# Seven products for four pairs of k tiles in every unit of the projections and the MLP, plain pieces between them, and the residual kept in device memory

## The chip, the cores and the metric

The kernel runs on one core of a Trainium2 chip. The core has five engines that run side by side, each through its own instructions in order: TensorE (PE, matrix products), VectorE (DVE), ScalarE (ACT), GpSimd (POOL), SyncE (SP, which here only issues transfers). They work on an on-chip memory of 128 partitions; matmul results go to PSUM, of which a bank holds 128x512 float32. The metric is the time of one execution on the device in microseconds, the slowest core's, here the only one's.

## The reference

One block of a model on 256 rows of 2048 columns, in float32: a mixer of two branches (a gated linear recurrence and chunked attention), merged by two sigmoid gates, an output projection and an MLP with squared ReLU, each with a residual.

```python
z = u @ w_in                                   # u = rms_norm(x); queries, keys, values, gates
gate_a, gate_b = jnp.split(jax.nn.sigmoid(gates), 2, axis=-1)
merged = gate_a * (y_a @ w_branch_a) + gate_b * (y_b @ w_branch_b)
h = x + merged @ w_out
u = rms_norm(h, norm_mlp_w)
h = h + jnp.square(jax.nn.relu(u @ w_up)) @ w_down    # w_up 2048x8192, w_down 8192x2048
return rms_norm(h, norm_final_w)
```

## The kernel before

**Products in three passes.** A float32 operand is split into a rounded high part and the rest (`split`, L88 to L90: a cast on ScalarE, a subtraction on VectorE), and a product is three matmuls, high x high, high x low and low x high (`mm3`, L142 to L145). A weight piece holds two k tiles of 128 rows by 512 columns, 128x1024 on the chip; `piece` (L643) loads it on the SP queue, `parts` (L658) splits it. Before a matmul can run, its piece must have landed in a buffer `raw`, gone through the cast into `wh` and through the subtraction into `wl`.

**Stages.** The recurrence and the attention come first (to about 395 us) and are not touched. From there on the work is cut into 21 *units*, calls of `gemm_s` (L689), each a product of 256 rows (two halves m) with 2048 k rows (16 k tiles) and 1024 columns (two halves n): three for gates (`ga2`, `gb0`, `gb2`), then after the branch products (`gemm2`, L675, not units) two for the output projection (`wo0`, `wo2`), and four times, for a quarter of the MLP's width, two up (`up00`, `up02`, then `up10` and so on) and two down (`dn00`, `dn02`). A unit's four results (m, n), called 11, 12, 21, 22, gather in four banks; there are six banks (`ps_k`).

**Seven products for eight.** A unit plain is 2 x 2 x 16 triples of matmuls, 192. For a pair of k tiles (k, k + 4) the rows' halves, the columns' halves and the two k tiles make a 2 x 2 by 2 x 2 block product, done with seven products in place of eight (Winograd's form of Strassen's method). It needs four sums of left-hand blocks (S5, S4, S2, S7, made by `combos`, L586, with their own splits) and four sums of weight blocks, made in place in the raw buffers on VectorE (`add`, L711; `less`, L716). The banks exchange partial results: a bank is begun as a copy of another (`begun`, L747), and copies u1, u2 of bank 21 (`copy`, L744) are subtracted from 12 and 22 later (`more`, L756). The parameter r tells how many pairs are so done: 4 in the down units, 3 in the gates, in wo0 and in seven up units, 2 in wo2 and up00. With r = 3 the third pair comes in half pieces (X, Y). The rest of the k tiles go plain, `plains`, for both m and one n at a time. One plain piece (the last) is left to the next unit (`late`, `flush`).

**Order and buffers.** Tile, the layer below, orders each engine's instructions at build time by a priority and puts in the waits. Splits, weight sums, copies and evictions are raised (`tc.high_priority(offset=2000)`); transposes of the next stage's operand and the left-hand sums (`h_blocks`, `turns`, `turned`, handed in as `steps` and taken up at points of the unit) are not. Raw buffers are eight (six in `wpool`, two in `xp`), split halves six each. A unit loads its blocks W11, W12, W22, W21 first and each plain piece where it is used, all on SP's queue. Row tiles of 128x512 ("tokens", `token`, L575, 17 of them) hold gates, copies u1 and u2, MLP rows on their way and, from L949 on, the eight tiles of the residual h, in place to the end: x is loaded, `evict` (L685) adds the output projection on VectorE, and the down units' results go through ScalarE into a token y and are added into h by a transfer that accumulates, on POOL's queue (L1000). The last quarter's results are evicted into h directly, and then come the final norm and the stores.

Of the kernel before, what the change touches and what calls it, by code (L numbers as in the profile page):

```python
# [50 lines left out]
def tile_hybrid_block(  # L51
# [455 lines left out]
    TOK = 17  # L507
# [67 lines left out]
    def token(what):  # L575
        return tk.tile([P, NC], F32, name=what, tag="t", bufs=TOK)

# [6 lines left out]
    R = 3  # L584

    def combos(lhs, what, home, blocks=None, n=R):  # L586

        a = blocks
        if not a:
            a = []  # L590
            for m in range(NM):
                for j in range(2):
                    t = tk.tile([P, R, P], F32, name=f"a{m}{j}_{what}", tag="t", bufs=TOK)
                    x = lhs[j][:, :R, :, m * P:(m + 1) * P].bitcast(F32)
# [12 lines left out]
        for two in ((5, s5), (4, s4)), ((2, s2), (7, s7)):  # L607
            if n > R:
                more = tk.tile([P, 2, 2, P], F32R, name=f"S{two[0][0]}m_{what}", tag="t", bufs=TOK)
            for q, (i, s) in enumerate(two):  # L610
                t = (tk if home == "a" else xp).tile([P, R, 2, P], F32R, name=f"S{i}_{what}", tag=f"S{i}{home}", bufs=1)
                split(t[:, :, 0, :], t[:, :, 1, :], s[:, :R])
                made[i] = [[t[:, k, u, :] for u in range(2)] for k in range(R)]
                if n > R:
                    split(more[:, q, 0, :], more[:, q, 1, :], s[:, R])
                    made[i].append([more[:, q, u, :] for u in range(2)])
        return made

    Sx = combos(xT, "x", "a")
# [9 lines left out]
    xp = ctx.enter_context(tc.tile_pool(name="xpool", bufs=1, reuse_waits="tile"))  # L629
    ps_k = ctx.enter_context(tc.tile_pool(name="ps_k", bufs=6, space=PSUM, reuse_waits="tile"))  # L630
# [3 lines left out]
    taken = {t: 0 for t in BUFS}  # L634

    def buf(tag, dtype, what):

        old, new = BUFS[tag]
        first = taken[tag] % (old + new) < old
        taken[tag] += 1  # L640
        return (wpool if first else xp).tile([P, 2 * NC], dtype, name=f"{tag}_{what}", tag=tag, bufs=old if first else new)

    def piece(w, what, *halves):  # L643

        raw = buf("raw", F32, what)
        (n0, k0), (n1, k1) = halves
        ncols = w.shape[-1]
        kpr = 4 * NC // ncols
        if n0 == n1 and k1 == k0 + 1 and k0 // kpr == k1 // kpr:
            src = w[n0 // ncols:(n0 + NC) // ncols, k0 // kpr, :, k0 % kpr:k0 % kpr + 2, :].rearrange("c p a n -> p c a n")  # L650
            nc.sync.dma_start(raw.rearrange("p (c a n) -> p c a n", a=2, n=ncols), src)
            return raw, ncols < NC
        for i, (n, k) in enumerate(halves):
            nc.sync.dma_start(raw[:, i * NC:(i + 1) * NC].rearrange("p (c n) -> p c n", n=ncols),
                              w[n // ncols:(n + NC) // ncols, k // kpr, :, k % kpr, :].rearrange("c p n -> p c n"))
        return raw, False

    def parts(raw, what, half=None):  # L658

        raw, turned = raw  # L660
        made = [buf(t, F32R, what) for t in ("wh", "wl")]
# [4 lines left out]
        if half is not None:  # L666
            dst, src = [t[:, half * NC:(half + 1) * NC] for t in made], raw[:, half * NC:(half + 1) * NC]
# [7 lines left out]
    def gemm2(lhs, w, n0, nkt, what):  # L675

        acc = [bank(f"{what}{m}") for m in range(NM)]
        for k in range(0, nkt, 2):
            wh, wl = parts(piece(w, f"{what}{k}", (n0, k), (n0, k + 1)), f"{what}{k}")
# [9 lines left out]
    def gemm_s(lhs, S, w, n0, what, done, r=R, kt0=0, steps=(), start=4, fresh=False, tail=False):  # L689

        n1 = n0 + NC
        steps = list(steps)
        points = [0]

        def point():
            points[0] += 1  # L700
            if points[0] > start and steps:
                steps.pop(0)[1]()

        c = {}
        load = lambda name, *halves: piece(w, f"{what}{name}", *[(n, kt0 + k) for n, k in halves])
        groups = (0, 2) if r == 4 else (0,)
        four = lambda name, n, k: [load(f"{name}{g}", (n, k + g), (n, k + g + 1)) for g in groups]

        def add(dst, t):
            with tc.high_priority(offset=2000):  # L710
                nc.vector.tensor_tensor(dst, dst, t, op=ALU.add)  # L711

        def less(dst, s, t):

            with tc.high_priority(offset=2000):
                nc.vector.tensor_tensor(dst, s, t, op=ALU.subtract)  # L716

        half = lambda W, i: W[0][:, i * NC:(i + 1) * NC]

        def mm(i, lh, ps, *tiles):  # L720

            first = i not in c
            if first:
                c[i] = bank(f"{what}c{i}")
            wh, wl = ps
            for a, k in tiles:
                mm3(c[i], *lh(k), wh[:, a], wl[:, a], first, False)
                first = False

        def mms(i, lh, Ws, name):  # L730
            for g, W in zip(groups, Ws):
                if g:
                    point()
                mm(i, lh, parts(W, f"{what}{name}{g}"), (0, g), (1, g + 1))

        def of(m, jj):
            return lambda k: lhs_of(lhs, k + 4 * jj, m)

        def comb(i):
            return lambda k: S[i][k]  # L740

        def copy(dst, i):
            with tc.high_priority(offset=2000):
                nc.scalar.copy(dst, c[i])  # L744
            return dst

        def begun(i, j):  # L747

            c[i] = bank(f"{what}c{i}")
            if fresh:  # L750
                nc.tensor.matmul(c[i], lhs[0][:, 0, 0, 0:P], lhs[0][:, 0].rearrange("p u t -> p (u t)"), start=True, stop=False, skip_group_check=True)
            copy(c[i], j)

        def more(i, t, op):
            with tc.high_priority(offset=2000):
                nc.vector.tensor_tensor(c[i], c[i], t, op=op)  # L756


        W11 = four("11", n0, 0)
        if r == 3:  # L760
            X = load("x", (n0, 2), (n1, 6))
        W12 = four("12", n1, 0)
        if r == 3:
            Y = load("y", (n0, 6), (n1, 2))
        W22 = four("22", n1, 4)
        W21 = four("21", n0, 4)
        points[0] = -2
        mms("11", of(0, 0), W11, "p1")
        if r == 3:
            px = parts(X, f"{what}px")  # L770
            mm("11", of(0, 0), px, (0, 2))
        begun("21", "11")
        for a, b in zip(W12, W11):
            add(a[0], b[0])
        mms("22", comb(5), W12, "p5")
        if r == 3:
            add(half(Y, 1), half(X, 0))
            py = parts(Y, f"{what}py")
            mm("22", comb(5), py, (1, 2))
        begun("12", "22")  # L780
        flush()

        points[0] = 0
        mms("12", comb(4), W22, "p3")
        for a, b in zip(W22, W12):
            add(a[0], b[0])
        if r == 3:
            mm("12", comb(4), px, (1, 2))
            add(half(X, 1), half(Y, 1))
        point()  # L790
        if r == 3:
            mm("11", of(0, 1), py, (0, 2))
        mms("11", of(0, 1), W21, "p2")
        for a, b, d in zip(W12, W22, W11):
            less(a[0], b[0], d[0])
        point()

        mms("21", comb(2), W22, "p6")
        if r == 3:
            mm("21", comb(2), parts(X, f"{what}px2", 1), (1, 2))  # L800
        u1 = copy(token(f"u1_{what}"), "21")
        point()

        def plain(n, *ks, raw=None):
            while steps and steps[0][0] <= ks[-1] // 4:
                steps.pop(0)[1]()
            raw = raw or load(f"r{n}_{ks[0]}", *[(n0 + n * NC, k) for k in ks])
            p = parts(raw, f"{what}r{n}_{ks[0]}")

            def m_half(m):  # L810
                for a, k in enumerate(ks):
                    mm3(c["12"[m] + "12"[n]], *lhs_of(lhs, k, m), p[0][:, a], p[1][:, a], False, k == KD - 1)

            return m_half

        def plains(n, *pairs):
            for ks in pairs:
# [249 lines left out]
```

## Time and profile before

| | |
|---|---|
| median of 3 runs | 1432.34 us (1432.34 to 1434.09) |
| span of the profiled execution | 1432.3 us |
| that execution's granted TensorE clock | 0.998 of full speed |
| moved by transfers | 279.17 MB, 195 GB/s on average |
| stages in that execution | first gate unit from 427 us, branch products from 554, wo0 from 643, up00 from 727, dn00 from 815; last matmul at 1422 |

"Span" is from the first to the last instruction. In the tables of groups a line names the code line, the engine, the operation, out<-in with shapes, the count, then busy time, the mean duration in ns and the idle time before it with what ended it. A tile's name carries its unit (`wh_dn00p`: high part of a product piece in unit dn00; `r` for a plain piece). Matmuls are pipelined: one lasts 0.39 us in the records while the next starts earlier, so their rate is read from their starts.

### The profile page before, as it was taken

What the parts mean: (1) busy time and instruction counts of PE and PEld (TensorE: products, weight loads), DVE (VectorE), ACT (ScalarE), POOL (GpSimd) and SP (SyncE); (2) the same over time, 40 slices, a digit from 0 to 9 for tenths busy, and PEclk for the clock granted to TensorE, in tenths of its full rate; (3) what the DMA queues carried; (4) which work ended last, traced back from release to release, by engine and by line L of the source; (5) the groups of instructions that cost most, each with busy time, mean ns of one, the idle gap of its engine ahead of it and who ended that gap; (6) DMA issues with size and microseconds to landing.
All of it is one profiled execution on the core that took longest, in us unless ns stands there. A gap on an engine that the chain in (4) does not pass through costs nothing.

```text
span 1432.3 us, 18448 instructions
## 1 busy us (share of the span) xinstructions
PE 1403.7 (98%) x6607; PEld 1155.6 (81%) x6607; DVE 1146.5 (80%) x1485; ACT 890.6 (62%) x1172; POOL 58.0 (4%) x120
## 2 busy tenths in 40 slices
PE   9999999999999999999999999999999999999997
PEld 7888788878788888888888877888778887888785
DVE  7779887675767874688987888888888888879886
ACT  6766744464656664445667766677666875667754
POOL 2000101010100000000000000000000000000000
PEclk9999999999999999999999999999999999999999
DMA  9654444555556656646663467854678535876433
GB/s 311 236 191 148 138 160 138 188 169 174 155 172 221 235 194 214 211 161 234 212 200 125 171 221 229 261 176 136 227 235 264 188 126 196 255 264 234 165 129 134
DMA packets 121003, 279.17 MB, mean 195 GB/s; under 512 B 10048, under 2 KB 31296, under 8 KB 120528
## 3 DMA queue, kind: packets, MB, share of 16 engines
q1 hardware_dynamic: 114720, 264.80, 54.6%
q0 software_dynamic: 5040, 11.60, 3.9%
q10 hardware_dynamic: 1152, 1.60, 0.3%
q8 instruction: 52, 0.85, 0.2%
q14 instruction: 39, 0.32, 0.1%
HBM read 269.57 MB, written 2.10 MB: 190 GB/s over the span
## 4 chain that ended last, share of the span: by engine, by line
PE 82%; DVE 6%; DMA 6%; ACT 2%; issue 2%; POOL 0%; SPq 0%; POOLq 0%; DVEq 0%; ACTq 0%
PE acc_ak L171 2%; PE acc_aq L171 2%; PE acc_hf L171 1%; DMA raw_hf<-in_w_in_t_dram 1%; PE ps L395 1%; PE acc_hq L171 1%; PE acc_bb L144 1%; PE acc_ba L144 1%; PE acc_av L145 1%; PE acc_ba L145 1%; PE acc_bb L143 1%; PE acc_bb L145 1%; PE acc_ba L143 1%; PE acc_av L143 1%; PE acc_av L144 1%
## 5 line engine op out<-in xcount | busy, mean ns | idle before, releaser
L711 DVE TENSOR_TENSOR raw_dn<-raw_dn,raw_dn 128x1024 f32<-128x1024 f32 x48 | 58.1, 1218 | 3.1 <-DMA raw_dn<-in_w_down_dram 2.8
L171 PE MATMUL acc_hf<-act_x,wh_hf 128*128 128x512 f32 x128 | 47.7, 409 | 1.1 <-DVE f L179 1.1
L171 PE MATMUL acc_aq<-act_x,wh_aq 128*128 128x512 f32 x128 | 47.7, 407 | 0.0
L171 PE MATMUL acc_hq<-act_x,wh_hq 128*128 128x512 f32 x128 | 45.7, 397 | 0.0
L171 PE MATMUL acc_ak<-act_x,wh_ak 128*128 128x512 f32 x128 | 45.0, 397 | 0.0
L711 DVE TENSOR_TENSOR raw_up<-raw_up,raw_up 128x1024 f32<-128x1024 f32 x24 | 29.3, 1222 | 14.5 <-DMA raw_up<-in_w_up_dram 14.2
L1000 POOL DMA_DIRECT2D h<-y x24 | 20.5, 853 | 477.8 <-ACT y L999 477.1
L170 PE MATMUL acc_aq<-act_x,wl_aq 128*128 128x256 f32 x120 | 35.1, 293 | 0.0
L170 PE MATMUL acc_hf<-act_x,wl_hf 128*128 128x256 f32 x120 | 34.4, 286 | 0.0
L90 DVE TENSOR_TENSOR wl_ga<-raw_ga,wh_ga 128x1024 fp32r<-128x1024 f32 x16 | 19.6, 1226 | 18.1 <-ACT wh_ga L89 16.4
L90 DVE TENSOR_TENSOR wl_av<-raw_av,wh_av 128x1024 fp32r<-128x1024 f32 x16 | 19.6, 1224 | 18.1 <-ACT wh_av L89 18.1
L170 PE MATMUL acc_ak<-act_x,wl_ak 128*128 128x256 f32 x120 | 33.6, 280 | 0.0
L170 PE MATMUL acc_hq<-act_x,wl_hq 128*128 128x256 f32 x120 | 33.6, 280 | 0.0
L90 DVE TENSOR_TENSOR wl_ba<-raw_ba,wh_ba 128x1024 fp32r<-128x1024 f32 x16 | 19.6, 1224 | 16.6 <-ACT wh_ba L89 16.6
L89 ACT CAST wh_ba<-raw_ba 128x1024 fp32r<-128x1024 f32 x16 | 16.9, 1053 | 24.3 <-PE acc_ba L145 10.0
L89 ACT CAST wh_bb<-raw_bb 128x1024 fp32r<-128x1024 f32 x16 | 16.9, 1054 | 22.8 <-PE acc_ba L145 11.1
L89 ACT CAST wh_av<-raw_av 128x1024 fp32r<-128x1024 f32 x16 | 16.8, 1053 | 22.0 <-PE acc_av L145 12.4
L90 DVE TENSOR_TENSOR wl_bb<-raw_bb,wh_bb 128x1024 fp32r<-128x1024 f32 x16 | 19.6, 1222 | 13.3 <-ACT wh_bb L89 13.3
L89 ACT CAST wh_aq<-raw_aq 128x1024 fp32r<-128x1024 f32 x16 | 16.8, 1049 | 20.9 <-PE acc_aq L171 8.8
L90 DVE TENSOR_TENSOR wl_aq<-raw_aq,wh_aq 128x1024 fp32r<-128x1024 f32 x16 | 19.6, 1224 | 12.5 <-ACT wh_aq L89 12.2
L171 PEld LDWEIGHTS acc_hf<-act_x,wh_hf 128*128 128x128 f32 x128 | 24.2, 189 | 6.2 <-DVE f L179 1.4
L171 PEld LDWEIGHTS acc_hq<-act_x,wh_hq 128*128 128x128 f32 x128 | 24.0, 188 | 5.4
(1291 smaller groups left out, 5162.6 us busy)
## 6 DMA issues: line engine op xcount, KB each, us to landing
raw_dn<-in_w_down_dram SPq DMA_DIRECT2D x64, 512.0 KB, 5.5
raw_up<-in_w_up_dram SPq DMA_DIRECT2D x32, 512.0 KB, 7.0
raw_ga<-in_w_in_t_dram SPq DMA_DIRECT2D x20, 512.0 KB, 4.1
raw_hi<-in_w_in_n_dram SPq DMA_DIRECT2D x16, 512.0 KB, 4.0
raw_hg<-in_w_in_n_dram SPq DMA_DIRECT2D x16, 512.0 KB, 3.6
raw_aq<-in_w_in_t_dram SPq DMA_DIRECT2D x16, 512.0 KB, 4.4
raw_ak<-in_w_in_t_dram SPq DMA_DIRECT2D x16, 512.0 KB, 3.9
raw_av<-in_w_in_n_dram SPq DMA_DIRECT2D x16, 512.0 KB, 4.2
```

The source lines that it names most:

```text
L89: (copy or nc.scalar.copy)(hi, src)
L90: nc.vector.tensor_tensor(lo, src, hi.bitcast(F32), op=ALU.subtract)
L143: nc.tensor.matmul(acc, hi, wh, start=first, stop=False, skip_group_check=True)
L144: nc.tensor.matmul(acc, hi, wl, start=False, stop=False, skip_group_check=True)
L145: nc.tensor.matmul(acc, lo, wh, start=False, stop=last, skip_group_check=True)
L170: nc.tensor.matmul(acc[:, cb, 0:T], wl[:, c], r[:, 0, :], start=False, stop=False)
L171: nc.tensor.matmul(acc[:, cb, :], wh[:, c], r.rearrange("p u t -> p (u t)"), start=kt == 0, stop=kt == nkt - 1)
L395: nc.tensor.matmul(ps[:, m, :], klf[:, a * P:(a + 1) * P], qrf[:, a * 192:(a + 1) * 192], start=True, stop=True)
L711: nc.vector.tensor_tensor(dst, dst, t, op=ALU.add)
L1000: nc.gpsimd.dma_start(r, t, accum_op=ALU.add)
```

## The change

Every unit now does four pairs with seven products; r is gone, with the half pieces. A unit is an object (`Unit`) so that the next unit's loads can be issued while the current one runs, and `run` is the hand-written order: products of the blocks A (W11 first), B, C, D with plain pieces between them, loads at fixed places, and two plain pieces (`LATE`) left for the next unit, taken after its first and second product. The weight sums are made with the blocks as A+B, B+C, A+C, D+A, each in place on VectorE in two passes of 128x1024 (`sums` and `sent` have the same body).

```diff
-    TOK = 17
+    TOK = 11
...
-    BUFS = {"raw": (6, 2), "wh": (4, 2), "wl": (4, 2)}
...
+        last = taken[tag] % 5 == 0
+        return (xp if last else wpool).tile([P, 2 * NC], F32R, name=f"{tag}_{what}", tag=tag, bufs=1 if last else 4)
...
+        pool, bufs = {"raw": (wpool, 6), "rawd": (xp, 2), "rawp": (xp, 3)}[tag]
...
+    LATE = [(12, 13), (14, 15)]
+    ITEMS = [(1, (8, 9)), (1, (10, 11)), (0, (8, 9)), (0, (10, 11)), (0, (12, 13)), (0, (14, 15))] + [(1, ks) for ks in LATE]
...
+        for _ in range(3 - sum(type(k) is tuple for k in u.raw)):
+            item(u)
+        u.product("11", "A", u.block(0, 0), True)
+        u.sums("A", "B")
+        u.begun("21", "11")
+        u.sent("B", "C")
+        q()
+        item(u)
+        u.bank("22")
+        u.product("22", "A", u.comb(5), True)
+        u.sums("A", "C")
+        u.begun("12", "22")
+        q()
+        item(u)
+        u.steps = list(u.make_steps())
+        u.product("12", "C", u.comb(4))
+        u.product("11", "D", u.block(0, 1))
+        u.sent("D", "A")
+        u.plain(1, (8, 9))
+        item(u)
+        u.product("21", "A", u.comb(2))
+        u1 = u.copy(token(f"u1_{u.what}"), "21")
+        if then:
+            then.load("A")
+        u.plain(1, (10, 11))
+        u.less("12", u1)
+        item(u)
+        u.product("21", "B", u.comb(7))
+        u2 = u.copy(token(f"u2_{u.what}"), "21")
+        if then:
+            then.load("B")
+            then.load("C")
+        u.plain(0, (8, 9))
+        u.less("22", u2)
+        item(u)
+        u.plain(0, (10, 11))
+        item(u)
+        u.product("21", "D", u.block(1, 1))
+        if then:
+            then.load("D")
+        u.plain(0, (12, 13))
+        item(u)
+        u.plain(0, (14, 15))
+        item(then)
+        u.end(0)
```

Between these lines stand calls `u.step(next(at))` (left out here), at which one pending step may be taken up; `item(x)` issues the load of the next plain piece in the order of `ITEMS`; `q()` takes one piece left over from the unit before. `plain` still takes up every step whose operand it needs. The combinations S of all four k tiles are now made at once (`combos` without `n`), in pools of their own, S_h in one that takes the place of eight gate tiles (`tkb`).

The residual is no longer held on the chip:

```diff
+    hd = [[dp.tile([P, NC], F32, name=f"hd{n}{m}", tag=f"hd{n}{m}") for m in range(NM)] for n in range(4)]
...
+    def h_out(m, n, acc):
+        t = token(f"h1_{n}_{m}")
+        with tc.high_priority(offset=2000):
+            nc.gpsimd.dma_start(t, x[m * P:(m + 1) * P, n * NC:(n + 1) * NC])
+        evict(t, acc)
+        nc.gpsimd.dma_start(hd[n][m], t)
+        h1[n][m] = t
...
-                nc.gpsimd.dma_start(r, t, accum_op=ALU.add)
+                nc.gpsimd.dma_start(hd[n][m], t, accum_op=ALU.add)
...
+                fin[m] = apool.tile([P, D], F32, name=f"fin{m}", tag="act")
+                for n in range(4):
+                    nc.gpsimd.dma_start(fin[m][:, n * NC:(n + 1) * NC], hd[n][m])
```

The loads back into `fin` are a last step of unit dn30; the last results are evicted into `fin`.

More of the change, by code (lines that the diff above doesn't have):

```diff
@@ L582, in sigmoid, with fours, combos @@
         return gate
-    R = 3
-    def combos(lhs, what, home, blocks=None, n=R):
+    def fours(t):
+        return t.rearrange("p (k t) -> p k t", t=P)
+    def combos(lhs, what, home, blocks=None):
         a = blocks
@@ L606, in combos @@
         made = {}
[L607 to L616, printed above, removed]
+        for i, s in ((5, s5), (4, s4), (2, s2), (7, s7)):
+            t = home.tile([P, 4, 2, P], F32R, name=f"S{i}_{what}", tag=f"S{i}", bufs=1)
+            split(t[:, :, 0, :], t[:, :, 1, :], s)
+            made[i] = [[t[:, k, u, :] for u in range(2)] for k in range(4)]
         return made
-    Sx = combos(xT, "x", "a")
+    Sx = combos(xT, "x", tk)
     ga, gb = [], []
@@ L882, in tile_hybrid_block @@
+    units = []
     for gates, c, col, what, fresh in ((ga, 2, C_GA, "ga", True), (gb, 0, C_GB, "gb", True), (gb, 2, C_GB, "gb", False)):
-        gates += [[None] * NM for _ in range(2)]
         def done(m, n, acc, gates=gates, c=c, what=what):
-            gates[c + n][m] = sigmoid(token(f"gate_{what}{c + n}{m}"), acc, m)
-        gemm_s(xT, Sx, w_in_t, col + c * NC, f"{what}{c}", done, fresh=fresh)
+            while len(gates) <= c + n:
+                gates.append([None] * NM)
+            gates[c + n][m] = sigmoid(token(f"gate_{what}{c + n}{m}", tkb if (what == "ga") == (c == 2) else None), acc, m)
+        units.append(Unit(lambda: xT, lambda: Sx, w_in_t, col + c * NC, f"{what}{c}", done, fresh=fresh))
@@ L889, in tile_hybrid_block @@
+    for u, then in zip(units, units[1:] + [None]):
+        run(u, then)
     flush()
@@ L958, in tile_hybrid_block @@
     NQ = 4
+    units = [Unit(lambda: mT, lambda: Sm, w_out, n0 * NC, f"wo{n0}", lambda m, n, acc, n0=n0: h_out(m, n0 + n, acc),
+                  steps=(lambda: h_blocks(0)) if n0 else (lambda: turned(mT, 3, "m3", ga)), start=3 if n0 else 0) for n0 in (0, 2)]
+    fin = {}
     for qd in range(NQ):
@@ L986, in done, with out_of @@
                 rs[c + n, m] = t
[L988 to L995 removed]
+            units.append(Unit(lambda: hT, lambda: Sh, w_up, qd * (FF // NQ) + c * NC, f"up{qd}{c}", done,
+                              steps=(lambda turns=turns: turns(0)) if c else (lambda: ()) if qd else (lambda: h_blocks(2)), start=3))
+        def out_of(m, n, acc, last=last, qd=qd):
             if not last:
```

336 lines of the change are left out of this document (140 added, 196 removed).

## The prediction

> **What bounds the kernel now.** I began with the page: its first rows, then the chain of work that ended last.
>
> ```profile
> span 1432.3 us, 18448 instructions
> PE 1403.7 (98%) x6607; PEld 1155.6 (81%) x6607; DVE 1146.5 (80%) x1485; ACT 890.6 (62%) x1172; POOL 58.0 (4%) x120
> PE 82%; DVE 6%; DMA 6%; ACT 2%; issue 2%; POOL 0%; SPq 0%; POOLq 0%; DVEq 0%; ACTq 0%
> ```
>
> TensorE (PE) is busy for 98% of the span and is 82% of the chain. A busy row can hide gaps, since one matmul is shown for 0.39 us while the next has already started. So next I read the timeline of PE alone, from 900 to 905 us; of its 24 rows these are the first and the last.
>
> ```profile
> 899.69 0.39 PE L145 MATMUL acc_dn02c<-wh_dn02r,act_u 128*128 128x512 f32 x1
> ...
> 904.90 0.39 PE L144 MATMUL acc_up10c<-wl_up10px,act_h 128*128 128x512 f32 x1
> ```
>
> 23 steps in 5.21 us: one matmul of 128x512 starts every 0.2265 us, with no gap, across the border of two units. That is the price of a matmul here. [...]
>
> Third, busy time by stretches cut at the units' borders (columns: stretch; length; busy time and count of PE, weight loads, VectorE = DVE, ScalarE = ACT, POOL; granted clock; DMA share; GB/s). Units, in order: wo2, up00, up02, dn00, dn02, up10, up12, dn10, dn12, then dn20, dn30 and the end.
>
> ```profile
> 683.00:727.00 44.00, 44.00 (x204) 36.59 (x204) 41.33 (x50) 28.16 (x39) 0.00 (x0) 1.00 0.60 192
> 727.00:771.00 44.00, 44.00 (x203) 36.46 (x202) 35.81 (x40) 28.88 (x39) 1.63 (x1) 1.00 0.55 179
> 771.00:815.00 44.00, 44.00 (x202) 36.12 (x202) 38.81 (x45) 34.22 (x49) 0.00 (x0) 1.00 0.55 192
> 815.00:861.00 46.00, 43.16 (x196) 34.74 (x195) 37.75 (x36) 30.20 (x36) 1.79 (x2) 1.00 0.54 188
> 861.00:903.00 42.00, 41.39 (x182) 33.66 (x181) 37.46 (x36) 26.64 (x30) 3.38 (x4) 1.00 0.73 226
> 903.00:945.00 42.00, 42.00 (x186) 34.47 (x185) 32.87 (x32) 26.59 (x31) 1.69 (x2) 1.00 0.66 219
> 945.00:988.00 43.00, 42.84 (x197) 35.17 (x196) 37.87 (x45) 34.24 (x49) 0.00 (x0) 1.00 0.58 196
> 988.00:1034.00 46.00, 44.35 (x201) 35.67 (x200) 38.50 (x37) 29.80 (x36) 1.70 (x2) 1.00 0.54 189
> 1034.00:1076.00 42.00, 41.55 (x182) 33.79 (x181) 37.19 (x36) 26.53 (x30) 3.40 (x4) 1.00 0.75 226
> 1161.00:1206.00 45.00, 43.96 (x200) 35.53 (x199) 38.30 (x37) 30.04 (x36) 1.70 (x2) 1.00 0.55 193
> 1332.00:1378.00 46.00, 44.23 (x201) 35.63 (x200) 40.17 (x40) 30.50 (x38) 0.00 (x0) 1.00 0.51 183
> 1422.00:1432.00 10.00, 0.45 (x2) 0.02 (x1) 3.21 (x7) 3.39 (x6) 0.81 (x2) 0.76 0.57 210
> ```
>
> Three readings. The wo and up units have no PE idle to speak of: only fewer matmuls shorten them. The dn units, which already use seven products for 4 pairs, do: 2.84, 1.65, 1.04 and 1.77 us in dn00, dn10, dn20 and dn30, 0.61 and 0.45 in dn02 and dn12. And VectorE is not far behind: 41.33 of 44 us in wo2 with PE full.
>
> Fourth, why the dn units wait. The chain in order of time shows a load between two VectorE steps in the same place of every one.
>
> ```profile
> 830.01 1.23 DVE wl_dn00r L90
> 831.25 7.38 DMA raw_dn00r<-in_w_down_dram
> ...
> 870.87 5.42 DMA raw_dn02r<-in_w_down_dram
> ...
> 1006.79 7.67 DMA raw_dn10r<-in_w_down_dram
> ...
> 1043.74 5.26 DMA raw_dn12r<-in_w_down_dram
> ```
>
> The eight raw buffers are all held by the four weight blocks of the unit, so a plain piece is asked for only when one comes free, and lands 5 to 8 us later. There is a second cause, in the waits of PE:
>
> ```profile
> PE acc_dn00c L143 <- ACT u_dn L744: 1.5, 1, 1.5
> PE acc_dn30c L143 <- ACT u_dn L744: 1.0, 1, 1.0
> PE acc_dn20c L143 <- ACT u_dn L744: 0.8, 1, 0.8
> ```
>
> Products into the same bank follow one another, and the second waits for the copy of the bank (u1, u2).
>
> **The change, part by part.**
>
> *Matmuls.* A unit takes 192 matmuls plain; each pair of k tiles done with seven products saves 3. Before: gates 3 units of 3 pairs, wo0 3, wo2 2, up00 2, seven up units 3, eight dn units 4: 69 pairs. After: 21 x 4 = 84. 15 pairs x 3 = 45 matmuls fewer, x 0.2265 = **-10.2 us**. This is on the path: PE ran these units without a gap. Nothing else of PE changes (transposes and the four matmuls that open a bank in the first two units stay).
>
> *Order and buffers.* Now three places (rawp) are kept for plain pieces, two (rawd) for block D, six for A, B, C, and a plain piece stands between products that share a bank. A piece is asked for when the third before it has been split. In matmul time (a product or a plain piece is 12 matmuls, 2.72 us), two plain pieces three apart in the new order are never closer than 10.9 us, against these landings:
>
> ```profile
> raw_dn<-in_w_down_dram SPq DMA_DIRECT2D x64, 512.0 KB, 5.5
> raw_up<-in_w_up_dram SPq DMA_DIRECT2D x32, 512.0 KB, 7.0
> h<-y POOLq DMA_DIRECT2D x24, 256.0 KB, 3.5
> ```
>
> The SP queue is in order, so the next unit's A waits behind the piece (0,(14,15)), and B, C, D behind others: by my count 12 of a unit's 16 pieces, 6.3 MB, are asked for within about 22 us, 286 GB/s if it were to land in it; the dn02 stretch moves 226 GB/s on average at a DMA share of 0.73. It is tight but ends some 10 us before the last of them is needed. So the dn waits should go: idle in dn00 to dn30 is 7.3 us, in dn02 and dn12 1.06, so about 2.1 for all four dn?2: at most -9.4. I take **-8**; bounds 0 and -9.4.
>
> *VectorE.* A split has one pass on ACT and one on VectorE, a weight sum one on VectorE. Back to back they cost less than their duration:
>
> ```profile
> 818.65 2.35 DVE L90 TENSOR_TENSOR wl_dn00p<-raw_dn,wh_dn00p 128x1024 fp32r<-128x1024 f32 x2
> 820.92 1.22 DVE L711 TENSOR_TENSOR raw_dn<-raw_dn,raw_dn 128x1024 f32<-128x1024 f32 x1
> ```
>
> 2.27 us for two, 1.135 each. A unit of 3 pairs has 20.5 splits and 6 sums (counted in 1024 columns), one of 2 pairs 19 and 4, one of 4 pairs 22 and 8. Added: 11 x (1.5 + 2) + 2 x (3 + 4) = 52.5 passes, 59.6 us. The left-hand sums S_x, S_m, S_h grow from 384 to 512 columns:
>
> ```profile
> 807.70 0.55 DVE L90 TENSOR_TENSOR S_u<-a_u,S_u 128x384 fp32r<-128x384 f32 x1
> ...
> 840.94 0.68 DVE L90 TENSOR_TENSOR act_u<-tp_u,act_u 128x512 fp32r<-128x512 f32 x1
> 841.54 2.35 DVE L90 TENSOR_TENSOR wl_dn00r<-raw_dn00r,wh_dn00r 128x1024 fp32r<-128x1024 f32 x2
> ```
>
> about 12 instructions each, by 0.13 us, 4.7 us in all. So VectorE goes from 1146.5 to about 1211 us. What lies beside matmuls costs nothing; where it exceeds PE's own time it is on the path. PE needs 180 x 0.2265 = 40.8 us for a unit and about 1.5 more for 16 transposes (four started within 0.38 us):
>
> ```profile
> 841.77 0.63 PE L106 MATMUL tp_u<-ident,r 128*128 128x128 f32 x4 [1.18 <-DVE act_u L90]
> 842.15 0.48 PE L145 MATMUL acc_dn00c<-wh_dn00r,act_u 128*128 128x512 f32 x1
> ```
>
> For wo2, up00, up02 VectorE needs 41.33 + 35.81 + 38.81 = 115.95, plus 7.9 + 7.9 + 4.0 for the added passes and 1.6 for S_h, 137.4 us. PE needs 3 x 42.3 = 126.9. VectorE is short by **10.5 us** there. What covers it is its lead. The first cast of dn00 and the first matmul that reads it:
>
> ```profile
> 807.05 1.05 ACT L89 CAST wh_dn00p<-raw_dn 128x1024 fp32r<-128x1024 f32 x1 [1.67 <-PE acc_up02c L145]
> ...
> 814.96 0.39 PE L143 MATMUL acc_dn00c<-wh_dn00p,act_u 128*128 128x512 f32 x1
> ```
>
> The splits are now 8 us ahead with six buffers of each half, some 6 us with the five of the new kernel. Left over: 4.5; with uneven demand inside a unit (the products lie in its first two thirds, and with sums they need 4.5 us of VectorE per 2.7 of PE) I take **+6**; bounds 0 (all lead, and idle slots that no row shows) and +10.5. From up10 on, a group of four units needs 32.87 + 37.87 + 38.50 + 37.19 = 146.4, plus 8, 154 us, against 166.2 of PE: it fits, at 93%, which is what wo2 does today without a PE wait. Inside a group up?2 is even (41.9 to 42.3) and dn?0 has room (38.5), so I add nothing.
>
> *ScalarE* gets 22.5 more casts of about 1.05 us, 24 us on 890.6. It stays under 36 us in a unit: hidden by PE.
>
> *Residual in device memory.* Eight loads of x move from ahead of the unit to its end; eight stores and eight loads back are added on POOL's queue, 24 adding transfers keep their count and change their target. POOL is busy 4%, an issue costs 0.85 us:
>
> ```profile
> L1000 POOL DMA_DIRECT2D h<-y x24 | 20.5, 853 | 477.8 <-ACT y L999 477.1
> ```
>
> Queued behind a store is the next load of x, and behind that the eviction of a bank. With six banks the next unit needs the third 5.4 us after its start, and the nearest landing is 3.5 us: hidden, 0; if the cover is gone, two units by about 3 us, +6. The eight final loads are issued in the middle of dn30 and needed at its end. The tail after the last matmul (1422 to 1432) is the same work: 0. Eleven instead of 17 tokens, of which eight held the residual: 0, up to +3 in wo2, where sums and residual meet.
>
> **Sum**, against the execution profiled, whose span of 1432.3 us is also the median of the runs shown: 1432.3 - 10.2 - 8 + 6 = **1420 us**.
>
> **Rivals.** (B) *VectorE never shows*: the lead covers all, 1432.3 - 10.2 - 9.4 = 1413. For it: 94% VectorE without a PE wait in wo2. Against: 137 us of demand in 127.
>
> (C) *The new order does not help*: units of 4 pairs cost what dn units cost now. dn02 and dn12 last 42 us, as up10 does; dn00 and dn10 46, against 43 to 44 of up02 and up12. Then wo and up gain nothing, the gates keep their 9 matmuls (-2.0), the wo2 stretch gives +1: about 1431. For it: same instructions as today's dn units. Against: their waits are from buffers that the change splits up. It comes out nearly the same if PE's stream has slack, so that fewer matmuls save nothing: 1432.3 - 8 + 6 = 1430. Against that: in wo2, without a gap, weight loads took 36.59 of 44 us, 83%, so a share near 81% is what a full stream shows. [...]
>
> (D) *The left-hand sums come late* (slower). Splits and weight sums are flagged urgent, S_h and S_u are not. With the four subtractions of the turned blocks S_u is twelve VectorE passes of 128x512, 0.60 us each from start to start (840.94 to 841.54 in the rows on the left-hand sums), about 7.2 us, and the second product of the next unit waits for them. If VectorE gets to them only once splits are far ahead, PE stands for those 7.2 us at five places (up00, dn00, dn10, dn20, dn30): 36 us, and 1432.3 - 10.2 - 8 + 36 = 1450. It decides from the point where VectorE has under 7 us to spare in the 30 us between the transposes and that product: by my count about 24 of those 30 are urgent, so it is close. For it: up02 at 42.5 of 42.3 us. Against: up12 today makes S_u in the same place with 37.87 of 43 busy and no PE idle beyond 0.16.
>
> **Chances.** Forecast 0.42, with its own range 1414 to 1428; B 0.2; C 0.14; D 0.24, spread from 1436 to 1455. 0.2% (2.9 us) is about what can be told from no change here. Faster: forecast, B and some of C, 0.66; within 0.2%: most of C, 0.1; slower: D, 0.24. The range takes in B's lower edge and the lower half of D: 1409 to 1444.
>
> **What would show it.** Right: 45 fewer matmuls of 128x512 at a pitch of 0.2265; PE idle in dn units under 0.5 us each; VectorE near 1211 us; PE waits on VectorE in wo2 to up02 or early in dn00, and few after 900 us. The loads row should drop out of the chain in the dn units. Wrong: PE waiting for S_u or S_h at a unit's second product (D), for raw loads (C), or for x at the end of a wo unit. A pitch below 0.2265 or VectorE under 1190 us would mean that I have the work wrong.

## The result and the profile after

The changed kernel takes 1425.82 us (median of 4 runs, 1425.17 to 1426.15), the kernel before, run beside it, 1432.36 us (1432.34 to 1434.09): ratio 0.9944, 95% interval 0.993 to 0.9958. It is faster by 6.5 us. The profiled execution has a span of 1424.1 us at a mean clock of 0.994; all sums below are against it.

The first rows of the page of the changed kernel, and its chain of work that ended last:

```profile
span 1424.1 us, 18284 instructions
PE 1392.0 (98%) x6562; PEld 1150.6 (81%) x6562; DVE 1203.9 (85%) x1494; ACT 915.0 (64%) x1173; POOL 63.9 (4%) x136
PE 90%; DVE 5%; DMA 2%; ACT 2%; issue 1%; POOL 0%; POOLq 0%; SPq 0%; ACTq 0%; DVEq 0%
```

45 matmuls fewer, as counted ahead. VectorE works 57.4 us more (64 were estimated). Transfers fell from 6% of the chain to 2%: the loads of plain pieces between two VectorE steps, which stood in it in every dn unit, are gone. Busy time by stretches, cut at the first product of each unit (wo2, up00, up02, dn00, dn02, up10, up12, dn10, and a stretch inside wo2 that is used further down):

```profile
678.00:730.60 52.60, 45.36 (x198) 36.79 (x197) 50.26 (x57) 31.89 (x42) 4.41 (x9) 0.94 0.58 200
730.60:780.00 49.40, 44.77 (x198) 36.39 (x197) 43.67 (x46) 30.96 (x40) 2.71 (x5) 0.97 0.57 192
780.00:822.80 42.80, 42.78 (x198) 35.36 (x197) 42.04 (x44) 35.23 (x47) 0.00 (x0) 1.00 0.58 197
822.80:865.60 42.80, 42.80 (x198) 35.30 (x197) 39.17 (x38) 30.80 (x38) 0.30 (x1) 1.00 0.60 197
865.60:906.40 40.80, 40.80 (x182) 33.78 (x181) 36.09 (x33) 26.98 (x30) 3.49 (x5) 1.00 0.80 232
906.40:947.20 40.80, 40.80 (x182) 33.78 (x181) 36.09 (x33) 27.55 (x31) 3.07 (x4) 1.00 0.80 232
947.20:990.00 42.80, 42.78 (x197) 35.36 (x196) 42.02 (x44) 35.20 (x47) 0.00 (x0) 1.00 0.59 197
990.00:1032.80 42.80, 42.80 (x198) 35.31 (x197) 39.16 (x38) 30.82 (x38) 0.29 (x1) 1.00 0.59 196
...
717.40:721.50 4.10, 3.98 (x9) 3.14 (x10) 3.00 (x5) 2.03 (x3) 0.00 (x0) 0.50 0.50 170
```

The kernel falls in two. From up02 on, a unit lasts 40.8 us, or 42.8 to 43.0 with its 16 transposes, which is 180 matmuls (and the transposes) all but without a gap; dn00 was 46 before. (The last unit, which runs its late pieces itself, takes 46.0.) But wo2 and up00, which lasted 44.0 us each, now last 52.6 and 49.4 with fewer matmuls. What PE waits for there, and in the first gate unit, from the view of waits of PE (total us, times, longest):

```profile
PE acc_wo2c L143 <- ACT u_wo L707: 7.2, 2, 4.9
...
PE tp_h L106 <- DVE hw L928: 3.6, 1, 3.6
PE acc_ga2c L144 <- DVE wl_ga2p11D L90: 1.5, 1, 1.5
...
PE acc_up00c L144 <- DVE wl_up00p21A L90: 1.0, 1, 1.0
```

The longest names ScalarE, and the copies u1 and u2 of bank 21. The timelines of ScalarE, VectorE and PE around it show whose delay it is. ScalarE:

```profile
706.87 0.61 ACT L930 ACTIVATE hsq<-h 128x512 f32<-128x512 f32 x1
...
707.78 1.22 ACT L89 CAST act_h<-hw 128x512 fp32r<-128x512 f32 x2 [0.20 <-DVE hw L928]
708.90 0.58 ACT L707 COPY u_wo<-acc_wo2c 128x512 f32<-128x512 f32 x1
713.18 1.34 ACT L89 CAST S_h<-a_h 128x512 fp32r<-128x512 f32 x2 [3.70 <-DVE a_h L601]
...
716.37 0.62 ACT L89 CAST S_h<-a_h 128x512 fp32r<-128x512 f32 x1 [0.37 <-DVE a_h L607]
716.89 0.58 ACT L707 COPY u_wo<-acc_wo2c 128x512 f32<-128x512 f32 x1
```

VectorE over the same time:

```profile
707.06 1.28 DVE L928 TENSOR_TENSOR hw<-tp_h,vt 128x512 f32<-128x512 f32 x2
...
710.06 1.89 DVE L597 TENSOR_TENSOR a_h<-act_h 128x512 f32<-128x512 f32 x3
...
715.65 0.69 DVE L607 TENSOR_TENSOR a_h<-a_h 128x512 f32<-128x512 f32 x1
```

PE:

```profile
712.20 0.39 PE L145 MATMUL acc_wo2c<-wh_wo2p21B,S_m 128*128 128x512 f32 x1
717.52 0.79 PE L143 MATMUL acc_wo2c<-wh_wo2r,act_m 128*128 128x512 f32 x1 [4.93 <-ACT u_wo L707]
718.12 0.63 PE L144 MATMUL acc_wo2c<-wl_wo2r,act_m 128*128 128x512 f32 x1
718.54 0.63 PE L145 MATMUL acc_wo2c<-wh_wo2r,act_m 128*128 128x512 f32 x1
...
721.53 0.53 PE L143 MATMUL acc_wo2c<-wh_wo2r,act_m 128*128 128x512 f32 x1
721.89 0.40 PE L144 MATMUL acc_wo2c<-wl_wo2r,act_m 128*128 128x512 f32 x1
```

Each copy is a 0.58 us instruction that stands in ScalarE's order behind casts of the turned rows and of S_h, and those casts wait for VectorE (hw, a_h). VectorE makes them only now because splits and weight sums went ahead. So the bank is filled at 712.6 (712.20 + 0.39), its copy is taken at 716.9, and PE, which must not write into bank 21 before, stands for 4.93 us. In up00 the transposes wait in the same way for hw, with splits of VectorE back to back ahead of it:

```profile
751.33 2.35 DVE L90 TENSOR_TENSOR wl_up00p21B<-raw_up00B,wh_up00p21B 128x1024 fp32r<-128x1024 f32 x2
753.60 1.22 DVE L90 TENSOR_TENSOR wl_up00r<-rawp_up00r,wh_up00r 128x1024 fp32r<-128x1024 f32 x1
754.73 1.28 DVE L928 TENSOR_TENSOR hw<-tp_h,vt 128x512 f32<-128x512 f32 x2
```

And after the 4.93 us nine matmuls start 0.427 us apart, at a granted clock of 0.50 (the last row of the stretches): the wait costs about 1.8 us more than it lasts, and the 3.58 us in up00 about 1.3 us.

*Stall* below is worked out from the starts of PE's matmuls: what a step to the next one lasts beyond 0.227 us (beyond 0.058 after a transpose, an allowance of the author's: transposes in a row start 0.109 us apart), steps over by less than 0.06 us left out. It counts gaps that a busy row hides, and the half clock. By it, the account of the 8.2 us between the two profiled executions, from the first product of one unit to that of another, is:

| stretch | before, us | after, us | matmuls fewer, x 0.2267 | left for waits |
|---|---|---|---|---|
| up to the gates, and the tail after the last matmul | 427.5 + 9.9 | 426.0 + 10.2 | 0 | -1.2 |
| gates to wo2 | 255.8 | 252.0 | 24: -5.4 | +1.7 |
| wo2, up00, up02 | 131.7 | 144.8 | 15: -3.4 | +16.5 |
| dn00 to the last matmul | 607.5 | 591.1 | 6: -1.4 | -15.0 |

(24 and 6 in place of 12 and 18, because two late pieces instead of one now cross the first and the last border. The part up to the gates is the same in the changed kernel and in all the edits of it below; it took 425.0 to 428.0 us in their profiled executions.) The sum of the last column from the gates on is +3.2: the change saved its 45 matmuls, took 15 us of waits out of the MLP, and put 18 us of new ones in, nearly all into two units.

### The profile page after: what moved, and what is told of

Read it like the earlier page. It is cut to its first block, busy times and chain, and to the rows that moved or that the text cites. A ratio compares the mean times of both kernels' runs of the same rounds, so it can differ in the third digit from the quotient of the medians.

```text
span 1424.1 us, 18284 instructions
## 1 busy us (share of the span) xinstructions
PE 1392.0 (98%) x6562; PEld 1150.6 (81%) x6562; DVE 1203.9 (85%) x1494; ACT 915.0 (64%) x1173; POOL 63.9 (4%) x136
## 4 chain that ended last, share of the span: by engine, by line
PE 90%; DVE 5%; DMA 2%; ACT 2%; issue 1%; POOL 0%; POOLq 0%; SPq 0%; ACTq 0%; DVEq 0%
PE acc_ak L171 2%; PE acc_aq L171 2%; PE acc_hf L171 1%; PE ps L395 1%; PE acc_hq L171 1%; PE tp_u L106 1%; PE acc_bb L143 1%; PE acc_av L143 1%; PE acc_ba L145 1%; PE acc_bb L145 1%; PE acc_ba L144 1%; PE acc_ba L143 1%; PE acc_av L144 1%; PE acc_bb L144 1%; PE acc_av L145 1%
## 5 line engine op out<-in xcount | busy, mean ns | idle before, releaser
L994 POOL DMA_DIRECT2D hd<-y x24 | 20.5, 854 | 468.1 <-ACT y L993 468.1
L90 DVE TENSOR_TENSOR wl_bb<-raw_bb,wh_bb 128x1024 fp32r<-128x1024 f32 x16 | 19.6, 1223 | 14.8 <-ACT wh_bb L89 14.8
L89 ACT CAST wh_av<-raw_av 128x1024 fp32r<-128x1024 f32 x16 | 16.8, 1053 | 22.0 <-PE acc_av L145 12.4
L89 ACT CAST wh_ba<-raw_ba 128x1024 fp32r<-128x1024 f32 x16 | 16.8, 1053 | 21.1 <-PE acc_bb L145 13.8
L89 ACT CAST wh_aq<-raw_aq 128x1024 fp32r<-128x1024 f32 x16 | 16.8, 1049 | 20.9 <-PE acc_aq L171 8.8
L171 PEld LDWEIGHTS acc_ak<-act_x,wh_ak 128*128 128x128 f32 x128 | 23.9, 188 | 5.5
L171 PEld LDWEIGHTS acc_aq<-act_x,wh_aq 128*128 128x128 f32 x128 | 24.2, 189 | 5.0 <-issue 0.7
```

The lines of the kernel that those rows point to most:

```text
L89: (copy or nc.scalar.copy)(hi, src)
L90: nc.vector.tensor_tensor(lo, src, hi.bitcast(F32), op=ALU.subtract)
L171: nc.tensor.matmul(acc[:, cb, :], wh[:, c], r.rearrange("p u t -> p (u t)"), start=kt == 0, stop=kt == nkt - 1)
L994: nc.gpsimd.dma_start(hd[n][m], t, accum_op=ALU.add)
```

## Experiments

The theory after the first trace: VectorE has too little time in wo2 and up00, and everything of theirs that is not flagged urgent (turned rows, S_h) comes late, and with it what ScalarE does behind it. Rivals: row tiles are held too early by the loads of x (*tokens*); the steps are taken up too early in wo2, and any other order would do (*order*). All kernels are edits of the changed one; ratios are to the kernel before on the same chip, and where two kernels' intervals overlap, the stalls are what tells them apart, each from one profiled execution. In the table a stall is put down to what PE ran just before it: a unit, by its tile, or a transpose (of any unit). Late pieces of wo2 run in up00's time; cut at the units' first products, the stalls of wo2 and up00 are 10.0 and 7.0 in the changed kernel, 0.4 and 14.0 in e2, 0.4 and 10.2 in e4. All in us:

| kernel | time | ratio, interval | wo2 | up00 | transposes, up02, dn00 | all from the gates on |
|---|---|---|---|---|---|---|
| before | 1432.36 | | 0.2 | 0.4 | 5.0 | 20.1 |
| changed | 1425.82 | 0.9944 (0.993 to 0.9958) | 10.0 | 6.8 | 1.4 | 23.9 |
| e1_xload | 1425.75 | 0.9943 (0.9926 to 0.9961) | 9.7 | 6.5 | 1.9 | 23.9 |
| e2_spread | 1422.05 | 0.9908 (0.9878 to 0.9938) | 2.8 | 9.3 | 3.4 | 21.3 |
| e12_both | 1422.24 | 0.9922 (0.9896 to 0.9948) | 2.8 | 7.8 | 3.6 | 19.7 |
| e3_nosums | 1411.14 | 0.9836 (0.9799 to 0.9872) | 2.6 | 0.4 | 1.7 | 9.9 |
| e4_hw | 1418.71 | 0.99 (0.9886 to 0.9915) | 1.8 | 7.4 | 2.5 | 17.3 |
| e5_two_wo2 | 1417.15 | 0.9893 (0.9875 to 0.9911) | 0.4 | 6.4 | 1.9 | 14.0 |
| e6_two_pairs | 1415.18 | 0.9876 (0.986 to 0.9893) | 0.4 | 0.5 | 5.6 | 12.2 |
| e8_fewer_wo2 | 1416.82 | 0.9884 (0.9866 to 0.9901) | 0.4 | 7.1 | 1.7 | 14.9 |
| e9_fewer_both | 1415.69 | 0.9879 (0.9862 to 0.9897) | 0.4 | 0.5 | 5.8 | 11.8 |
| e13_fewer_three | 1413.57 | 0.9858 (0.9829 to 0.9887) | 0.4 | 0.5 | 1.0 | 7.0 |
| e7_rawp2 | 1430.26 | 0.9971 (0.9959 to 0.9984) | 14.0 | 7.1 | 1.5 | 29.7 |
| e10_sums_gpsimd | 1428.94 | 0.997 (0.9957 to 0.9982) | 9.3 | 8.5 | 3.2 | 26.0 |

**e1_xload.** The load of x for the output tiles is no longer raised, so that it takes its row tile later.

```diff
-        with tc.high_priority(offset=2000):
-            nc.gpsimd.dma_start(t, x[m * P:(m + 1) * P, n * NC:(n + 1) * NC])
+        nc.gpsimd.dma_start(t, x[m * P:(m + 1) * P, n * NC:(n + 1) * NC])
```

> The load of x into a row tile for an output-projection result is no longer raised in priority, so that it takes its row tile only near the eviction that needs it. Tokens theory (in wo2 the copies u1 and u2 come late because 4 of the 11 row tiles are held by x some 20 to 30 us early): the PE wait on u_wo falls from 7.2 us to under 1.5, wo2 and up00 together from 102.0 us to 92 to 94, the kernel to 1416 to 1419. VectorE theory (its 94 us of work in wo2 and up00 against 85 us of PE sets their length): no change beyond 2 us, 1424 to 1427.

Time and stalls are those of the changed kernel, but the run does not decide: wo2's four loads of x are issued at 707.3 to 709.9 us in both traces, so the edit did not move them. What speaks against tokens is the trace of the changed kernel: nothing there waits for these loads, VectorE is busy back to back (its longest idle time from 692 to 717 us is 0.25 us), ScalarE's longest idle time, 3.70 us, ended with VectorE's a_h, and each copy follows the instruction before it at once.

**e2_spread.** The five steps that wo2 takes up (four turned blocks, then S_h) are no longer drawn forward by plain pieces, but taken one at a point.

```diff
-                  steps=(lambda: h_blocks(0)) if n0 else ...
+                  steps=(lambda: [(99, f) for _, f in h_blocks(0)]) if n0 else ...
```

> The five steps of wo2 (four blocks of h turned, then the left-hand sums S_h) are taken one at each later point of the unit, and not all five ahead of its first plain piece. Tokens theory: u1 asks for its row tile before the steps have taken eleven, so its wait (2.3 us) goes; u2 still comes after some, so the 4.9 us wait shrinks; 1418 to 1421. VectorE theory: the same work, so at most 2 us better, or worse by the S_h that now comes late for the second product of up00 (PE waits there): 1424 to 1428.

The waits for the copies are gone, and wo2's stall fell from 10.0 to 2.8. But up00's grew to 9.3, led by a new wait (view of waits of PE):

```profile
PE acc_up00c L143 <- ACT S_h L89: 4.4, 1, 4.4
```

That is rival D of the prediction, at one place. The time lies between the two that were expected. Order moves the wait and brings 3.8 us (2.9 of them in wo2 and up00 by the profiled executions); it does not remove it.

**e12_both**, e1 and e2 together.

> Both edits: x taken late, and the steps of wo2 one at a time. Tokens theory: no PE wait on u_wo, wo2 and up00 at 87 to 92 us, 1412 to 1416. VectorE theory: 1423 to 1427.

As e2; the loads of x are issued at the same points as there, so this run too tells nothing of tokens.

**e3_nosums.** The four weight sums of wo2 and up00 are left out, 16 passes of 128x1024 (18.2 us of VectorE); the products there run on the plain blocks. Matmuls, loads and order stay.

```diff
+        full = u.what not in ("wo2", "up00")
+        if full:
             u.sums("A", "B")
...
```

(and so for the other three sums.)

> The four weight sums are left out in units wo2 and up00 alone: 16 passes of 128x1024 fewer on VectorE, 18.2 us. Row tiles and order as they are. VectorE theory: wo2 and up00 fall from 102.0 us to about 86 to 88, the kernel to 1410 to 1412. Tokens theory: the PE waits on u_wo (7.2 us, and the slow clock after the longer one) stay, only the waits in up00 (5 us) go: 1418 to 1421.

14.7 us (1.0%) faster than the changed kernel, as VectorE's lack of time would have it. Of the waits in the two units one is left:

```profile
PE acc_wo2c L143 <- ACT u_wo L707: 2.0, 1, 2.0
```

With matmuls, transfers and order in place, only VectorE's work is less, and the stall of the two units falls from 16.8 to 3.0 us. This is the run that carries the theory. It also shortens the way from a load to its split, since no sum stands between; but of PE's named waits in these two units of the changed kernel only the one of 1.0 us was for the split of a summed block.

**e4_hw.** e2, and S_h made from the products hw (which are the blocks that it needs) instead of adding high and low parts again: four VectorE passes of 128x512 fewer in wo2.

```diff
+            if n < 2:
+                hw[m, n] = tmp
...
-        last = factor if n0 else lambda: Sh.update(combos(hT, "h", sp))
+        last = factor if n0 else lambda: Sh.update(combos(hT, "h", sp, [hw[m, j] for m in range(NM) for j in range(2)]))
```

> On top of the steps taken one at a time, S_h takes its four blocks from the products tp times w that are there anyway, and not from high plus low part added again: 4 passes of 128x512 fewer on VectorE (2.4 us), where it is short. VectorE theory: the wait for S_h in up00 shrinks by about that, 1418.5 to 1421 (1422.05 with the steps alone). If only the order counts: 1422.

The stalls fall by another 4.0 us from e2 (21.3 to 17.3), for 4 x 0.60 = 2.4 us less of VectorE (the mean granted clock of the profiled execution is 0.994 in e2 and 0.997 in e4); by the times the two can't be told apart (0.99 against 0.9908). up00 keeps 7.4 us of stall.

**e5_two_wo2 and e6_two_pairs.** wo2 alone, or wo2 and up00, go back to two pairs, as before; order and buffers stay new. A unit so treated has 6 matmuls more, and 3 splits and 4 sums fewer.

```diff
+            self.groups = (0,) if what in ('wo2', 'up00') else (0, 2)
...
-            for g, raw in zip((0, 2), self.raw[name]):
+            for g, raw in zip(self.groups, self.raw[name]):
...
+        if two:
+            u.plain(1, (2, 3))
...
```

(the second half of each block goes as a plain piece, for one n and both m, at four places of the order; the load of the next A moves behind them.)

> The same in wo2 alone. VectorE theory: 86 us of its work in the two units against 86.2 of PE, so the lead covers most and little waiting is left: 1411 to 1417; the slow clock should show in one of the two units at most. Other theory: wo2 keeps its late copies of bank 21: 1419 or more.

> Units wo2 and up00 go back to two pairs of k tiles with seven products, as before the change, in the new order and with the new buffers; their other 12 k tiles are plain. Six matmuls more in each (+2.7 us of PE in all), 3 splits and 4 weight sums fewer in each (15.9 us of VectorE in all). VectorE theory: its work in the two units falls to about 78 us, under PE's 87.5; their waits (17 us with the slow clock) go nearly all: 1411 to 1414. If it is not VectorE but the copies and the turned blocks that are in the wrong place, 5 us of waits or more stay: 1417 to 1421.

Each takes the stall out of the units it treats: e5 out of wo2 (0.4), e6 out of both (0.4 and 0.5). With 12 matmuls more, 2.7 us, e6 is about 10 us faster than the changed kernel. Neither time is quite as the theory had it: e5 keeps 6.4 us of stall in up00, and e6 is 1.2 us above its range. What is left in e6 comes later, in dn00:

```profile
PE acc_dn00c L143 <- ACT act_u L89: 1.2, 1, 1.2
PE acc_dn00c L145 <- DVE S_u L90: 1.2, 1, 1.2
```

**e7_rawp2.** Two places for plain pieces instead of three, the rest as changed.

```diff
-        pool, bufs = {"raw": (wpool, 6), "rawd": (xp, 2), "rawp": (xp, 3)}[tag]
+        pool, bufs = {"raw": (wpool, 6), "rawd": (xp, 2), "rawp": (xp, 2)}[tag]
```

> Two places instead of three for plain pieces. If the waits of the dn units went because a piece is asked for long ahead, they come back here, in every unit: a piece two ahead is 8.2 us of matmuls away, against a landing of 5.5 to 7 us and 2.3 us for its split. Then PE idle of 0.5 to 1.5 us a unit, 1433 to 1450. If the order alone removed them: 1425 to 1428.

In between: about 4 us slower than the changed kernel, nearly all of it in wo0 (1.9 us of stall for 0.5) and wo2 (14.0 for 10.0). The dn units stay without a gap (dn00 0.3). So the third place was not what took their waits away. That leaves two places apart from the blocks, and the new order; which of them did it was not separated.

**e8_fewer_wo2 and e9_fewer_both.** The edits of e4 on top of e5 and of e6.

> wo2 with two pairs as in e5_two_wo2, and the two edits of e4_hw on top (block steps spread, four passes of VectorE fewer). e5_two_wo2 left 6.4 us of stall in up00, 4.2 of them a wait of the transposes for the products hw; e4_hw left 1.8 in wo2 and 7.4 in up00. If what is left in up00 is VectorE's backlog carried over from wo2, the two together take most of the 6.4: 1411 to 1413. If it is up00's own demand (its sums, the S_h splits), about 4 us of it stay: 1415 to 1417.

> wo2 and up00 with two pairs as in e6_two_pairs, and the two edits of e4_hw on top. e6_two_pairs had no stall above 0.5 us in wo2 and up00 and 5 us at the start of dn00, where PE waited for S_u and a transposed block. If that wait is the backlog's last place, with less work for VectorE ahead of it it goes: 1410 to 1412. If S_u is late by the order of the steps in up02 alone, it stays: 1415.

Both miss what they were made for and come out as their second branch has it. e8 is no better than e5 (1416.82 against 1417.15): up00 keeps 7.1 us, and the wait is again for S_h, which the spread steps make last:

```profile
PE acc_up00c L145 <- DVE S_h L90: 3.5, 1, 3.5
```

In e9 the waits of e6 in dn00 stay as they were. Fewer passes in wo2 do not help a wait two units later; where its queue forms is not shown by this run.

**e10_sums_gpsimd.** The sums D+A of wo2 and up00, four of the sixteen passes, on GpSimd.

```diff
+            eng = nc.gpsimd if (dst, src) == ("D", "A") and self.what in ('wo2', 'up00') else nc.vector
...
-                    nc.vector.tensor_tensor(a[0], a[0], b[0], op=ALU.add)
+                    eng.tensor_tensor(a[0], a[0], b[0], op=ALU.add)
```

> The changed kernel with the sums D+A of wo2 and up00 on GpSimd instead of VectorE: 4 of the 16 passes. If VectorE's lack of time sets the loss in wo2 and up00, and GpSimd makes a pass of 128x1024 in under about 5 us without slowing VectorE, the 4.5 us it is relieved of show: 1420 to 1423. If the two engines slow each other, or the sum comes later than the product that needs it (seventh in the order for D+A, some 15 us after its inputs), 1426 or more. e3_nosums, without all 16, gave 1411.

Slower than the changed kernel by 3 to 4 us. GpSimd's timeline in wo2:

```profile
689.03 2.39 POOL L745 TENSOR_TENSOR rawd_wo2D<-rawd_wo2D,raw_wo2A 128x1024 f32<-128x1024 f32 x1 [0.38 <-DMA raw_up00A<-in_w_up_dram]
...
692.61 3.30 POOL L745 TENSOR_TENSOR rawd_wo2D<-rawd_wo2D,raw_wo2A 128x1024 f32<-128x1024 f32 x1 [0.67 <-DVE wl_wo2p11D L90]
```

and VectorE's:

```profile
689.47 3.05 DVE L90 TENSOR_TENSOR wl_wo2p11D<-rawd_wo2D,wh_wo2p11D 128x1024 fp32r<-128x1024 f32 x1
692.44 1.21 DVE L90 TENSOR_TENSOR wl_wo2r<-rawp_wo2r,wh_wo2r 128x1024 fp32r<-128x1024 f32 x1
693.57 3.42 DVE L90 TENSOR_TENSOR wl_wo2p21A<-raw_wo2A,wh_wo2p21A 128x1024 fp32r<-128x1024 f32 x1
```

A split of 1.21 us that starts while GpSimd adds takes 3.05 and 3.42 (the one at 692.44, which had started just before GpSimd, keeps its 1.21). In up00 a split took 3.43 us and a subtraction of S_h 2.82 in place of 0.69. That is 1.8 + 2.2 + 2.2 + 2.1, about 8 us lost, to be spared 4.5.

**e13_fewer_three.** As e6, and up02 with two pairs as well.

```diff
-            self.groups = (0,) if what in ('wo2', 'up00') else (0, 2)
+            self.groups = (0,) if what in ('wo2', 'up00', 'up02') else (0, 2)
```

> As e6_two_pairs (wo2 and up00 with two pairs), and up02 with two pairs as well: 6 more matmuls (1.4 us) and 7 passes of VectorE fewer in up02 (8 us). e6_two_pairs had no stall above 0.5 us in wo2 and up00, and 5 us in dn00, where PE waited for S_u and for a turned block. If the wait is VectorE's lack of time, now in up02, it goes with these passes: 1415.2 - 5 + 1.4, that is 1411 to 1413, with wo2, up00, up02 and dn00 all without a stall above 1 us. If S_u is late because of where it stands in VectorE's order (urgent splits and sums ahead of it), not for want of time, the wait stays and the time is 1416 to 1418.

1413.57 us, 1.4% under the kernel before, the fastest here with the whole computation. The stretches of wo2, up00 and most of up02:

```profile
677.00:732.00 55.00, 55.00 (x251) 45.39 (x250) 52.51 (x61) 34.45 (x47) 5.42 (x10) 1.00 0.70 238
732.00:780.00 48.00, 48.00 (x223) 39.45 (x222) 37.75 (x39) 33.55 (x47) 1.80 (x3) 1.00 0.58 198
780.00:822.00 42.00, 42.00 (x191) 34.88 (x190) 37.62 (x40) 29.73 (x39) 0.00 (x0) 1.00 0.54 177
```

PE has no wait left there (stalls of 0.4, 0.5 and 0.2 us by the starts), VectorE is at 95% in the first, and the wait for S_u is gone. The time is 0.6 us above the range expected. That speaks for want of time: e6's wait went with passes of VectorE, at an unchanged order. But up02 so treated also has four plain pieces more between its steps, so the run alone cannot rule out that they gave S_u its slot.

## Why the prediction was right, and where its sum was not

The forecast of 1420 us was 5.8 too low, inside the forecast's own range of 1414 to 1428; faster was the likelier sign. It came out through two errors of opposite sign: 7.0 us too little was expected from the dn units' waits going, and 12.2 too little as VectorE's cost. That the time fell inside the range is in part luck; that the kernel got faster through fewer matmuls and the end of those waits is not. Step by step, against the profiled execution (1424.1):

**Matmuls, -10.2.** Right: 45 fewer records, at the same pitch. In up30, without a stall in both kernels, 183 matmuls in 41.48 us (first product to the next unit's) became 180 in 40.80: 0.68 us, three pitches. In up10, also 180 in 40.80, weight loads are 83% of the time (33.78): the form of rival C in which PE's stream has slack falls.

**Waits in the dn units, -8.** Mis-sized: -15.0 from dn00 to the end. The mechanism was right (the load rows left the chain, the units run all but gap-free), but its size was taken from the idle that the stretches show, 7.3 and 2.1 us, and the bound of -9.4 with it. A matmul is shown for 0.39 us at a pitch of 0.2265, so each gap is shown 0.16 us too short and a small one not at all. The prediction says this of the page's first row, and then read the size from such rows. By the starts, the dn units of before lost 14.8 us, not 9.4, and the up units from up10 on 2.4; in the changed kernel these are 1.5 and 1.3. The reason given was also partly wrong: e7 shows that the third place for plain pieces is not needed for it.

**VectorE in wo2 to up02, +6.** This is the step that failed. The demand was right: 135.97 us of VectorE in the three stretches, 137.4 forecast; so was the place. What failed is the step from demand to time, "left over: 4.5", with 10.5 as its bound: it cost +16.5, and another +1.7 came ahead of it, nearly all in the first gate unit, which the sum left out. Of the 16.5, 7.6 are VectorE's shortage (135.97 less three times the 42.8 us of a unit without gaps), and the rest is time in which VectorE itself stood. Three things were not in the forecast's step. The lead of 6 us took nothing off that can be seen in this sum. The wait does not come where VectorE is short: the urgent splits were in time nearly everywhere, and late were the products hw and S_h, then ScalarE's casts of them, then the copies u1 and u2 queued behind those on ScalarE; so PE and VectorE in turn waited for each other, and VectorE stood for 8.8 of the 144.8 us (144.8 - 135.97) in which it was the short engine. The prediction named S_h and S_u as not urgent, but not what stands behind them on ScalarE. And about 3.1 us are half clock after the two long waits. The waits by name are 7.2 + 3.6 + 1.0 = 11.8; the clock and short gaps make the rest. e3 confirms the cause (-14.7 us without the 16 passes), and e6 and e13 agree with it.

**Even units fit at 98%.** Right: up02 and up12 have VectorE at 42.04 and 42.02 of 42.80 us and no wait of PE.

**Residual, 0.** Right: no wait of PE is for x, for the residual or for its last loads. The accumulating transfers cost as before (20.5 us, 854 ns each), and the tail after the last matmul is 10.2 us against 9.9:

```profile
L994 POOL DMA_DIRECT2D hd<-y x24 | 20.5, 854 | 468.1 <-ACT y L993 468.1
```

**Rivals.** B (VectorE never shows) falls in wo2 and up00. C (the order does not help) falls from up02 on. D (left-hand sums late) did not happen in the changed kernel, yet is real: e2, e8, e6 and e9 each show it, at one place, S_h in up00 or S_u in dn00, as soon as the earlier wait is removed. With the half clock it cost 9.4 us in e2, 7.0 in e8, and 4.3 and 4.5 in e6 and e9 (there half of it a wait for a turned block), where the prediction has 7.2 at each of five places. (Its 42.5 us for VectorE in up02 is 42.8 by its own rows, 38.81 + 4.0.)

**Open.** Whether the changed kernel could keep four pairs in all units with another order was not settled: every order tried left over 6 us in up00. No run moved the copies of bank 21 off ScalarE. The 2 us in the first gate unit (VectorE's split of block D) were not tried.

## What to carry to other kernels

When work is moved to an engine that is already near the bound, sum its demand unit by unit and leave the saving out where the demand exceeds the bounding engine's time: leaving three of the 21 units at two pairs (e13) more than doubled the gain. Look for the wait not at the urgent work but at what is not flagged, and at what is queued behind that on a third engine. Read the size of small gaps from the starts of a pipelined engine, not from its busy time (here a matmul is shown for 0.39 us at a pitch of 0.2265).

## What the runs showed of the hardware

**Half clock after a wait.** In the changed kernel nine matmuls ran 0.427 us apart after 4.93 us of PE idle, six after 3.58 us, at a granted clock of 0.50; after 2.31 us none did. The price of these two waits is 1.8 and 1.3 us. Their length does not decide it alone: in e6 six matmuls ran 0.43 us apart after two waits of 1.19 and 1.15 us whose ends lie 1.9 us apart (mean granted clock 0.98 from 780 to 830 us).

**GpSimd against VectorE.** An addition of 128x1024 on GpSimd took 2.39 to 3.30 us where VectorE takes 1.22, and a VectorE pass that started beside it was longer by some 2 us. The four lengthened passes end about their own length after GpSimd's: at 692.52 against 691.42 us and 696.99 against 695.91, and in up00 at 746.35 against about 745.3 and 749.09 against 748.54 (this one a pass of 0.69 us). In e10 the price, about 8 us of VectorE, was more than the 4.5 us of work that was moved.
